# Making the token-independent S5 tables earlier and keeping them in DRAM, in a three-branch decoder layer on one core

## The chip, the core and the metric

The kernel runs on one core of a Trainium2 chip. The metric is the device time of one execution in microseconds (us), the median of several runs. A profiled execution lists every instruction of the engines: PE (TensorE; PEld is its weight load), DVE (VectorE), ACT (ScalarE), POOL (GpSimd), SP (SyncE, which here issues every DMA).

## What is computed

One layer over 2048 tokens of width 1024, all in float32. `h = RMSNorm(x)` goes through one input projection of 8716 columns, which is split among an S5 branch (`u_a`, `z_a`), an attention branch (`q`, `k`, `v`, `z_b`), a Mamba-2 branch (`xbc`, `dt`, `z_c`) and three merge gates. The S5 branch is the one that the change is about:

```python
def s5_mixer(u, a_re, a_im, log_step, b_re, b_im, c_re, c_im, d, glu_w, glu_b):
    step = jnp.exp(log_step.astype(f32))[:, None]
    mag = jnp.exp(a_re * step)
    ang = a_im * step
    lam_re, lam_im = mag * jnp.cos(ang), mag * jnp.sin(ang)
    ...                                            # bb = discretized b
    bu_re = jnp.einsum('gpi,bsgi->bsgp', bb_re, ug)
    bu_im = jnp.einsum('gpi,bsgi->bsgp', bb_im, ug)
    ...                                            # h_t = lam h_(t-1) + bu_t, complex, over 2048 tokens
    y = jnp.einsum('gip,bsgp->bsgi', c_re, h_re) - jnp.einsum('gip,bsgp->bsgi', c_im, h_im)
    y = y.reshape(Bt, S, S5_WIDTH) + d.astype(f32) * u
    g = jax.nn.gelu(y)
    return g * jax.nn.sigmoid(g @ glu_w + glu_b)
```

There are 32 groups of 16 channels with 64 complex states each. The powers of lambda, the discretized b and the products made of them depend on parameters alone, on no token.

## The kernel before

**The projection is the backbone.** `main` walks through 272 units of PE work, 136 for each half of the tokens. First half: 40 units of `main_qkv` (units 0 to 39), 12 of `main_dtz`, 20 of `main_xbc`, 16 of `main_uz` (72 to 87) and 48 of `main_gates` (88 to 135). Second half: 16 of `main_uz` (136 to 151), 40 of `main_qkv` (152 to 191), then the rest. A unit is 48 products of 128x256 or 24 of 128x512. Each 256 columns of weights (1 MB) come by `wload` (L339, tile `wr`, one buffer), and `wsplit` (L353) splits them on ACT (`wh`, L360) and DVE (`wl`, L361) into high and low parts, with six buffers for the eight half-tiles that two weights would need.

**Branch work is spread between the units.** `run` gets jobs (a generator, its number of steps, first unit, last unit) and advances each in proportion as the units pass. The framework then orders every engine's instructions by a simulated timeline, so the order on an engine is fixed when the program runs. All DMAs are issued in order by SP. Branch tiles come from pools that are opened and closed with the phases (`jp0`, `jp1`, `jp2`); the PSUM tiles of branch work share five banks (`cps`, L250).

**The S5 path.** `s5_setup` (L857, units 2 to 38) computes per-group tables over 128 partitions (real and imaginary part times 64 states) and writes them to `tab_d`, [128, 32 groups, 163 columns], in ten pieces of 16 to 19 columns (L935, L940, L952, L967, L1015). A piece of 16 columns lies in `tab_d` as runs of 64 bytes, one for each partition and group, 4096 runs to a piece.

`s5` (L1028, units 153 to 180 beside the second half's `main_qkv`) works in eight blocks of four groups. `prep` loads the block's tables and channels `u`, makes `x1` and `o0` (`cplx`: two POOL products and one DVE addition of 128x512 each, L1042 to L1044), from `o0` the lag kernels (`kp` on PE L1062, `ks` L1066 to L1068), writes these to `ks_d` and loads them back as a Toeplitz matrix `t0`. The block then transposes `x1` into `p1` (L1082), makes `o1` by `cplx`, and for each pair of groups the phasor table `wt` (four POOL products L1102 and L1103, two DVE operations L1104). None of these reads a token. For each group follow the token operations: a product `inc` (L1112), three DVE operations on it and a POOL addition (L1116 to L1119), the scan over 256 chunks on DVE (L1121), three more DVE operations and a POOL addition (L1127 to L1130), and two products into `yp` (L1132, L1133).

Beside the first half's gates run `ssd(0)` (units 73 to 135), which makes its decay matrices on POOL (`sr`, L806), and `a0_early` (units 84 to 120).

Of the kernel before, what the change touches and what calls it, by code (L numbers as in the profile page):

```python
# [21 lines left out]
P = 128  # L22
# [6 lines left out]
TABW = 163  # L29
# [4 lines left out]
class Small:  # L34
    """float32 exp, sin/cos and softplus on small parameter arrays, by range reduction and polynomials."""
# [94 lines left out]
    def softplus(self, x, out=None):  # L130
        """max(x, 0) + log1p(exp(-|x|)), log1p(e) = 2 atanh(e / (2 + e))"""
# [18 lines left out]
class Hybrid:  # L150
# [3 lines left out]
    # ---------------------------------------------------------------- memory  # L154
    def setup(self, ctx):
# [28 lines left out]
        self.tab_d = dram("tab_d", [P, 32, TABW])  # L184
# [21 lines left out]
        # additive attention mask [query, previous block | current block]  # L206
# [46 lines left out]
    # ------------------------------------------------------------- h^T  # L253
# [15 lines left out]
    def norm_tile(self, tt, xh, w=None):  # L269
        """rows of a token tile over their RMS (times w), transposed, in two halves"""  # L270
# [48 lines left out]
    def a0_early(self):  # L319
        """h^T of the second half, kept in DRAM until its first half is used up"""  # L320
# [16 lines left out]
    # ------------------------------------------------------- weight tiles  # L337
# [11 lines left out]
    def wtile(self, name, specs):  # L349
        """columns [(c0, n), ...] of w_in as fp32r hi and lo parts, four K-pairs each."""  # L350
# [15 lines left out]
    def tok_unit(self, wt, tb, tt, n, ps):  # L366
        """ps[tokens, n] = h w for token tile tt of time block tb."""
# [9 lines left out]
    def ch_unit(self, wt, tb, m, ps):  # L377
        """ps[channels, 512 tokens] = (h w)^T for the 128 columns m of a weight tile."""
# [16 lines left out]
    # -------------------------------------------------- the input projection  # L395
# [36 lines left out]
    def silu2(self, nm, z, out, zin=None):  # L432
        """out = 2 silu(z) = (tanh(z/2) + 1) z"""
# [49 lines left out]
    def conv(self, ct, tb, ps):  # L483
        """causal depthwise conv (weights halved), silu, and both layouts to DRAM"""
# [108 lines left out]
    class AttBlock:  # L593
        """one block of 128 queries, four heads, against its own and the previous block of keys"""
# [44 lines left out]
        def scores(self):  # L639
# [5 lines left out]
            # even and odd heads sit in different row halves of the array: one bank for each  # L645
# [40 lines left out]
    def merge(self):  # L686
        """mix of the three head groups by their softmax denominators, gate, y_b^T"""
# [35 lines left out]
    # ------------------------------------------------------------------ SSD  # L723
    def ssd_dt(self, half):
# [21 lines left out]
        # exact two-part split of dt * a for the one-pass products  # L746
# [109 lines left out]
    # ------------------------------------------------------------------- S5  # L856
    def s5_setup(self):  # L857
        """per-group tables over partitions (re | im, state): powers of lambda, phasors of lambda^8,
        discretized b and c in both complex arrangements"""
# [13 lines left out]
        tab = self.tab_d  # L873
        T = {}
# [65 lines left out]
        nc.sync.dma_start(tab[:, :, 147:163], w.rearrange("p g a n -> p g (a n)"))  # L940
# [5 lines left out]
        for i in range(2):  # L946
# [5 lines left out]
            nc.sync.dma_start(tab[:, :, 64 + 16 * i:80 + 16 * i], o)  # L952
# [8 lines left out]
        for i in range(2):  # L961
            pt = self.cps([P, 4, P], f"s5ct{i}")
            for b in range(4):
# [42 lines left out]
            # one step to modulus one: v (3 - |v|^2) / 2  # L1006
# [21 lines left out]
    def s5(self):  # L1028
# [5 lines left out]
        def cplx(b, w, name, kr, ki, x1, x2, f):  # L1034
            """[lr_n x1 +- li_n x2] over eight powers and 16 columns"""
            o = self.ct(f"s5{name}{b}", [P, 4, 8, 16], tag="s5c", bufs=5)
            t = self.ct(f"s5{name}t{b}", [P, 4, 8, 16], tag="s5ct", bufs=2)

            def bc(k, x):
                return (w[:, :, k:k + 8].unsqueeze(3).to_broadcast([P, 4, 8, 16]),  # L1040
                        x.unsqueeze(2).to_broadcast([P, 4, 8, 16]))
            gp.tensor_mul(o, *bc(kr, x1))  # L1042
            gp.tensor_mul(t, *bc(ki, x2))
            f(o, o, t)  # L1044
            return o

        def prep(b):
            gs = slice(b * 4, b * 4 + 4)
            w = self.ct(f"s5t{b}", [P, 4, TABW], tag="s5tab", bufs=2)
            nc.sync.dma_start(w, self.tab_d[:, gs, :])  # L1050
            u = self.ct(f"s5u{b}", [P, 4, 256], tag="s5u", bufs=2)
            for j in range(8):
                nc.sync.dma_start(u[j * 16:(j + 1) * 16],
                                  self.ua_d[b * 64:(b + 1) * 64, j, :].rearrange("(g i) c -> i g c", i=16))
            b1, b2, d1, d2 = (w[:, :, k:k + 16] for k in (64, 80, 96, 112))

            x1 = cplx(b, w, "x", 147, 155, b1, b2, v.tensor_add)
            o0 = cplx(b, w, "k", 128, 137, d1, d2, v.tensor_add)
            # lag kernels, zeros before lag 0, as rows of a Toeplitz matrix
# [11 lines left out]
            t0 = self.ct(f"s5t0{b}", [P, 4, P], tag="s5t0", bufs=2)  # L1071
            for i in range(8):
                nc.sync.dma_start(t0[i * 16:(i + 1) * 16], self.ks_d[:, gs, (7 - i) * 16:(7 - i) * 16 + P])
            return w, u, x1, d1, d2, t0

        todo = [prep(0)]
        yield
        for b in range(8):
            w, u, x1, d1, d2, t0 = todo.pop()
            pp = self.cps([P, 4, P], f"s5pp{b}")  # L1080
# [362 lines left out]
```

## Time and profile before

| what | us |
|---|---|
| time, median of 3 runs (2604.53 to 2605.4) | 2605.06 |
| span of the profiled execution | 2611.2 |
| PE busy in it | 2477.1 (95%) |
| DVE busy in it | 1465.2 (56%) |
| POOL busy in it | 718.3 (28%) |

The page of the profile cuts the span into 40 slices of 65.3 us, and its digits are busy shares in tenths. PE is at 9 nearly everywhere; it falls to 7 or 8 in the first four slices and again from the eighteenth to the twenty-first, where DVE stands at 8 and 9:

```profile
PE   8778999999999999978889999999999999999999
DVE  6652255643433335488986546642333887878663
```

### The profile page before, as it was taken

To read this page: it belongs to the slowest core of one execution; us is meant where nothing else is said; L and a number is where in the kernel's file an instruction comes from. 1 tells how busy PE (TensorE), PEld (TensorE's weight loads), DVE (VectorE), ACT (ScalarE), POOL (GpSimd) and SP (SyncE) were. 2 spreads that over 40 slices of the span, in tenths; PEclk is the share of its full clock that TensorE was granted. 3 is DMA by queue.
4 is the path that set the end of the run, shared out by engine and by line. 5 is a ranking of instruction groups with operands and counts; after the bars stand their busy time and mean duration, and the time that the engine had idled before them with its cause. 6 is when DMAs were issued, how large, how long until landed. Compare 5 with 4: busy or idle time off the path is not lost. (4 is left out here: it accounts for less than half of the span.)

```text
span 2611.2 us, 40810 instructions
## 1 busy us (share of the span) xinstructions
PE 2477.1 (95%) x15216; PEld 2173.1 (83%) x15216; DVE 1465.2 (56%) x3153; ACT 888.8 (34%) x1956; POOL 718.3 (28%) x737
## 2 busy tenths in 40 slices
PE   8778999999999999978889999999999999999999
PEld 8778998888888888877789998888888779797888
DVE  6652255643433335488986546642333887878663
ACT  4122234543233224212225335443332433333331
POOL 2121000002333324288862100000010343534221
PEclk8988999999999999999999999999999999999999
DMA  7995332433445335343336432443343667675664
GB/s 156 90 56 117 100 108 83 138 117 108 134 145 158 119 103 166 81 111 106 101 97 198 127 119 90 138 138 105 117 137 123 212 201 218 200 214 169 204 201 133
DMA packets 463591, 354.90 MB, mean 136 GB/s; under 512 B 132641, under 2 KB 420641, under 8 KB 463393
## 3 DMA queue, kind: packets, MB, share of 16 engines
q1 hardware_dynamic: 463392, 352.29, 50.6%
q8 instruction: 121, 1.98, 0.3%
q14 instruction: 78, 0.63, 0.1%
HBM read 239.79 MB, written 112.41 MB: 135 GB/s over the span
## 5 line engine op out<-in xcount | busy, mean ns | idle before, releaser
L384 PE MATMUL ps_g<-hT_hi,wh_g 128*128 128x512 f32 x768 | 310.0, 404 | 0.0
L386 PE MATMUL ps_g<-hT_hi,wl_g 128*128 128x512 f32 x768 | 305.6, 398 | 0.0
L385 PE MATMUL ps_g<-hT_lo,wh_g 128*128 128x512 f32 x768 | 305.0, 397 | 0.0
L806 POOL TENSOR_TENSOR sr<-tle,ahl 128x384 fp32r<-128x384 f32 x128 | 116.3, 930 | 519.9 <-PE sd L811 388.5
L386 PEld LDWEIGHTS ps_g<-hT_hi,wl_g 128*128 128x128 f32 x768 | 144.5, 188 | 33.1
L385 PEld LDWEIGHTS ps_g<-hT_lo,wh_g 128*128 128x128 f32 x768 | 144.5, 188 | 32.3
L384 PEld LDWEIGHTS ps_g<-hT_hi,wh_g 128*128 128x128 f32 x768 | 144.4, 188 | 32.2
L1272 POOL TENSOR_TENSOR fm<-fm,fg 128x512 f32<-128x512 f32 x64 | 96.0, 1500 | 209.7 <-DVE fg L1270 172.6
L361 DVE TENSOR_TENSOR wl_g<-wr_g,wh_g 128x512 fp32r<-128x512 f32 x96 | 71.0, 759 | 116.1 <-ACT wh_g L360 106.3
L659 ACT ACTIVATE sm<-sm,ml 128x256 f32<-128x256 f32 (+1 forms) x192 | 86.4, 451 | 136.1 <-DVE ml L657 111.9
L373 PE MATMUL ps_q<-wh_q,hT_hi 128*128 128x256 f32 x384 | 112.5, 294 | 18.0 <-ACT e_q L424 17.6
L384 PE MATMUL ps_xbc<-hT_hi,wh_xbc 128*128 128x512 f32 x320 | 129.0, 403 | 0.0
L385 PE MATMUL ps_xbc<-hT_lo,wh_xbc 128*128 128x512 f32 x320 | 128.6, 402 | 0.0
L386 PE MATMUL ps_xbc<-hT_hi,wl_xbc 128*128 128x512 f32 x320 | 128.4, 401 | 0.0
L373 PE MATMUL ps_v<-wh_v,hT_hi 128*128 128x256 f32 x384 | 110.7, 291 | 13.2 <-ACT e_v L414 10.8
L374 PE MATMUL ps_v<-wl_v,hT_hi 128*128 128x256 f32 x384 | 112.9, 295 | 9.5 <-DVE wl_v L361 9.5
L563 ACT ACTIVATE e_g<-ps_g 128x512 f32<-128x512 f32 x96 | 56.9, 595 | 182.3 <-PE ps_g L386 173.8
L498 DVE SCALAR_TENSOR_TENSOR ac_cv<-xb_cv,convw,ac_cv 128x512 f32<-128x512 f32 x120 | 90.3, 752 | 48.9 <-ACT ac_cv L496 48.2
L374 PE MATMUL ps_k<-wl_k,hT_hi 128*128 128x256 f32 x384 | 112.0, 292 | 5.8 <-DVE wl_k L361 5.7
L374 PE MATMUL ps_q<-wl_q,hT_hi 128*128 128x256 f32 x384 | 112.5, 294 | 4.6 <-DVE wl_q L361 4.6
L373 PE MATMUL ps_k<-wh_k,hT_hi 128*128 128x256 f32 x384 | 112.1, 294 | 4.8 <-ACT e_k L424 4.8
L375 PE MATMUL ps_q<-wh_q,hT_lo 128*128 128x256 f32 x384 | 113.4, 296 | 3.3 <-DVE hT_lo L317 3.3
(627 smaller groups left out, 7552.5 us busy)
## 6 DMA issues: line engine op xcount, KB each, us to landing
wr_g<-in_w_in_dram SPq DMA_DIRECT2D x24, 1024.0 KB, 5.3
g_d<-e_g SPq DMA_DIRECT2D x96, 256.0 KB, 2.4
fg<-g_d SPq DMA_DIRECT2D x96, 256.0 KB, 5.3
or<-in_w_out_dram SPq DMA_DIRECT2D x16, 1024.0 KB, 5.8
fr<-in_proj_c_dram SPq DMA_DIRECT2D x32, 384.0 KB, 5.1
wr_xbc<-in_w_in_dram SPq DMA_DIRECT2D x10, 1024.0 KB, 5.4
x<-in_x_dram SPq DMA_DIRECT2D x32, 256.0 KB, 3.9
wr_uz<-in_w_in_dram SPq DMA_DIRECT2D x8, 1024.0 KB, 5.4
```

The source lines that it names most:

```text
L361: nc.vector.tensor_sub(l[:, :, :n], s, h[:, :, :n].bitcast(F32))
L373: nc.tensor.matmul(ps, hi[:, t], wh, start=kt == 0, stop=False)
L374: nc.tensor.matmul(ps, hi[:, t], wl, start=False, stop=False)
L375: nc.tensor.matmul(ps, lo[:, t], wh, start=False, stop=kt == KT - 1)
L384: nc.tensor.matmul(ps, wh, hi, start=kt == 0, stop=False)
L385: nc.tensor.matmul(ps, wh, lo, start=False, stop=False)
L386: nc.tensor.matmul(ps, wl, hi, start=False, stop=kt == KT - 1)
L498: nc.vector.scalar_tensor_tensor(acc, xb[:, k:k + 512], cw[:, ct, k:k + 1], acc, op0=ALU.mult, op1=ALU.add)
L563: nc.scalar.activation(e, ps, AF.Tanh, scale=0.5)
L659: nc.scalar.activation(sm[:, h], sm[:, h], AF.Exp, bias=ml[:, h:h + 1], accum_out=ob[:, h, 64:65])
L806: nc.gpsimd.tensor_mul(r, self.tle.unsqueeze(1).to_broadcast([P, 3, P]), ahl[:, i, h0:h0 + 3].unsqueeze(2).to_broadcast([P, 3, P]))
L1272: nc.gpsimd.tensor_add(acc, acc, gt)
```

## The change

**Longer runs.** `tab_d` becomes [128, 8 blocks, 4 x 162]: within a block each piece holds its four groups side by side, so a piece of 16 columns is written by `put` as 1024 runs of 256 bytes in place of 4096 of 64. The decay `rho` leaves the table and goes to `rho_d`, 128 runs of 128 bytes. There are as many table writes as before and the bytes are the same.

**Tables earlier.** The parameter part of `s5` becomes `s5_tables`, 40 steps in units 83 to 134, beside `main_gates` of the first half, `ssd(0)` and `a0_early`. It runs the same POOL, DVE, PE and ACT operations and writes `p1`, `o1` (256 KB a block each) and `wt` (1 MB a block) to new DRAM tensors; `ks_d` is written as before. The pool `jp1` of the first attention is closed at unit 82 and `jp1t` is opened in its place; the steps of `ssd(0)` keep their pace.

**What is left of `s5`.** It has 42 steps in units 153 to 180. `load` fetches `u` (8 DMAs), `p1`, `wt`, `t0` (8) and `o1`, two buffers each, one block ahead. The token operations on PE, DVE, POOL and ACT are the same, one yield for each group. Elsewhere only comments and docstrings went.

```diff
-TABW = 163
+TABW = 162
...
-        self.tab_d = dram("tab_d", [P, 32, TABW])
+
+        self.tab_d = dram("tab_d", [P, 8, 4 * TABW])
+        self.rho_d = dram("rho_d", [P, 32])
+        self.p1_d = dram("p1_d", [P, 32, P])
+        self.o1_d = dram("o1_d", [P, 32, P])
+        self.wt_d = dram("wt_d", [P, 32, 2, 256])
...
-        tab = self.tab_d
-        T = {}
+        def put(off, wd, src):
+            nc.sync.dma_start(self.tab_d[:, :, off * 4:(off + wd) * 4], src)
...
-        w = self.ct("s5w", [P, 32, 19])
+        nc.sync.dma_start(self.rho_d, rho)
+        w = self.ct("s5w", [P, 32, 18])
         nc.vector.tensor_copy(w[:, :, 0:9], lr)
         nc.vector.tensor_copy(w[:, :, 9:18], li)
-        nc.vector.tensor_copy(w[:, :, 18], rho)
-        nc.sync.dma_start(tab[:, :, 128:147], w)
+        put(128, 18, w.rearrange("p (b g) k -> p b (g k)", b=8))
         w = self.ct("s5wr", [P, 32, 2, 8])
         for n in range(8):
             nc.vector.tensor_copy(w[:, :, 0, 7 - n], lr[:, :, n])
             nc.vector.tensor_copy(w[:, :, 1, 7 - n], li[:, :, n])
-        nc.sync.dma_start(tab[:, :, 147:163], w.rearrange("p g a n -> p g (a n)"))
+        put(146, 16, w.rearrange("p (b g) a n -> p b (g a n)", b=8))
...
-            nc.sync.dma_start(tab[:, :, 64 + 16 * i:80 + 16 * i], o)
+            put(64 + 16 * i, 16, o.rearrange("p (b g) k -> p b (g k)", b=8))
...
-            nc.sync.dma_start(tab[:, :, 96 + 16 * i:112 + 16 * i],
-                              d.rearrange("p b (g i) -> p (b g) i", i=16))
+            put(96 + 16 * i, 16, d.rearrange("p a (h c) -> p (a h) c", h=2))
...
-                k = 32 * lev + 16 * i
-                nc.sync.dma_start(tab[:, :, k:k + 16], ph[i])
+                put(32 * lev + 16 * i, 16, ph[i].rearrange("p (b g) k -> p b (g k)", b=8))
...
-    def s5(self):
+    def s5_tables(self):
...
+        for b in range(8):
             gs = slice(b * 4, b * 4 + 4)
+            w = self.ct(f"s5t{b}", [P, 4 * TABW], tag="s5tab", bufs=2)
+            nc.sync.dma_start(w, self.tab_d[:, b, :])
...
+            x1 = cplx("x", rev[:, :, 0:8], rev[:, :, 8:16], b1, b2)
+            pp = self.cps([P, 4, P], f"s5pp{b}")
+            for g in range(4):
+                nc.tensor.transpose(pp[:, g, :], x1[:, g].rearrange("p n i -> p (n i)"), self.ident)
+            p1 = self.ct(f"s5p1{b}", [P, 4, P], tag="s5p1", bufs=1)
+            nc.scalar.copy(p1, pp)
+            nc.sync.dma_start(self.p1_d[:, gs, :], p1)
+            yield
+            o0 = cplx("k", pw[:, :, 0:8], pw[:, :, 9:17], d1, d2)
...
             nc.sync.dma_start(self.ks_d[:, gs, :], ks.rearrange("p g n i -> p g (n i)"))
             yield
+            o1 = cplx("o", pw[:, :, 1:9], pw[:, :, 10:18], d1, d2)
+            nc.sync.dma_start(self.o1_d[:, gs, :], o1.rearrange("p g n i -> p g (n i)"))
+            yield
             for pr in range(2):
...
                     gp.tensor_mul(v16(wt[:, :, q, :]), hi16(32), lo16(x))
                     gp.tensor_mul(v16(tmp), hi16(48), lo16(y))
                     f(wt[:, :, q, :], wt[:, :, q, :], tmp)
+                nc.sync.dma_start(self.wt_d[:, b * 4 + pr * 2:b * 4 + pr * 2 + 2], wt)
                 yield
+
+    def s5(self):
+        nc = self.nc
+        v, gp = nc.vector, nc.gpsimd
+        rho = self.ct("s5rho", [P, 32])
+        nc.sync.dma_start(rho, self.rho_d)
+
+        def load(b):
+            gs = slice(b * 4, b * 4 + 4)
...
+            u = t4("u", None, (P, 4, 256))
+            for j in range(8):
+                nc.sync.dma_start(u[j * 16:(j + 1) * 16],
+                                  self.ua_d[b * 64:(b + 1) * 64, j, :].rearrange("(g i) c -> i g c", i=16))
+            p1 = t4("p1", self.p1_d[:, gs, :])
+            wt = t4("w", self.wt_d[:, gs], (P, 4, 2, 256))
+            t0 = t4("t0", None)
+            for i in range(8):
+                nc.sync.dma_start(t0[i * 16:(i + 1) * 16], self.ks_d[:, gs, (7 - i) * 16:(7 - i) * 16 + P])
+            return u, p1, wt, t0, t4("o1", self.o1_d[:, gs, :])
+
+        todo = [load(0)]
+        yield
...
-        run([(self.ssd(0), 66, 73, 135), (chain(self.attention(0, 0), self.attention(1, 0)), 40, 41, 80),
-             (self.a0_early(), 8, 84, 120)], 136)
+        ssd0, early0 = self.ssd(0), self.a0_early()
+        run([(early(ssd0, 10), 10, 73, 82), (chain(self.attention(0, 0), self.attention(1, 0)), 40, 41, 80)], 82)
+        s2.close()
+        s2, self.jp = open_pool("jp1t")
+        run([(ssd0, 56, 83, 135), (self.s5_tables(), 40, 83, 134), (early0, 8, 84, 120)], 136)
         s2.close()
         s1.close()
         st, self.jp = open_pool("jp2")
-        run([(self.s5(), 66, 153, 180)], 180)
+        run([(self.s5(), 42, 153, 180)], 180)
...
```

## Rows read from the trace of the kernel before

**Rows 1.** The page's first lines: span; busy us, share and instructions of engines.

```profile
span 2611.2 us, 40810 instructions
PE 2477.1 (95%) x15216; PEld 2173.1 (83%) x15216; DVE 1465.2 (56%) x3153; ACT 888.8 (34%) x1956; POOL 718.3 (28%) x737
```

**Rows 2.** Busy by stretch: PE, PEld, DVE, ACT, POOL (instructions), PEclk, DMA share, GB/s.

```profile
60.00:110.00 50.00, 49.56 (x420) 49.36 (x420) 40.92 (x249) 11.60 (x20) 7.82 (x8) 1.00 1.59 84
110.00:220.00 110.00, 68.67 (x480) 67.64 (x479) 41.53 (x166) 17.68 (x31) 18.75 (x16) 0.78 1.08 83
...
640.00:960.00 320.00, 320.00 (x1518) 262.44 (x1518) 116.32 (x158) 93.20 (x192) 107.55 (x122) 1.00 0.42 129
...
1100.00:1360.00 260.00, 217.28 (x1529) 201.31 (x1528) 232.56 (x354) 59.84 (x116) 218.53 (x217) 0.94 0.37 98
...
2000.00:2535.00 535.00, 502.70 (x2781) 429.71 (x2780) 412.93 (x790) 201.89 (x468) 199.16 (x164) 0.97 0.66 203
```

**Rows 3.** The same view of two short stretches in which PE never idles.

```profile
280.00:290.00 10.00, 10.00 (x88) 10.00 (x87) 1.38 (x2) 2.42 (x4) 0.00 (x0) 1.00 0.13 32
1000.00:1020.00 20.00, 20.00 (x88) 16.18 (x87) 10.82 (x10) 6.68 (x9) 17.82 (x15) 1.00 0.59 159
```

**Rows 4.** Waits of ACT from 110 to 220 us: total, times, longest.

```profile
ACT wh_k L360 <- DMA wr_k<-in_w_in_dram: 32.4, 1, 32.4
ACT wh_q L360 <- DMA wr_q<-in_w_in_dram: 31.4, 1, 31.4
ACT wh_v L360 <- DMA wr_v<-in_w_in_dram: 24.9, 1, 24.9
```

**Rows 5.** DMA in the same stretch: packets, megabytes, rate, packets by size.

```profile
DMA packets 29220, 9.16 MB, mean 83 GB/s; under 512 B 21663, under 2 KB 29215, under 8 KB 29215
```

**Rows 6.** DMA issues of the whole run: count, KB each, median us to landing.

```profile
wr_uz<-in_w_in_dram SPq DMA_DIRECT2D x8, 1024.0 KB, 5.4
...
ua_d<-e_uz SPq DMA_DIRECT2D x16, 256.0 KB, 2.6
...
tab_d<-s5ph SPq DMA_DIRECT2D x4, 256.0 KB, 17.6
```

**Rows 7.** Waits of PE from 1100 to 1360 us: total, times, longest.

```profile
PE s5kp L1062 <- DVE s5k L1044: 13.8, 4, 6.6
PE s5i L1112 <- DVE s5mt L1118: 9.3, 7, 2.0
PE s5yp L1132 <- DVE s5mt L1118: 6.7, 5, 2.2
```

**Rows 8.** DVE groups there: shapes, count, busy us, mean ns, idle before.

```profile
L1121 DVE TENSOR_TENSOR_SCAN s5h<-s5t,s5m 128x256 f32<-128x256 f32 x30 | 32.3, 1077 | 4.7 <-POOL s5m L1119 4.4 <-POOL s5r L1126 0.3
L1104 DVE TENSOR_TENSOR s5w<-s5w,s5wt 128x512 f32<-128x512 f32 x28 | 30.5, 1088 | 4.2 <-POOL s5w L1102 4.0
...
L1116 DVE TENSOR_TENSOR s5m<-s5i,s5w 128x256 f32<-128x256 f32 x30 | 12.5, 415 | 0.5
...
L1068 DVE SCALAR_TENSOR_TENSOR s5ks<-ident,s5dd,s5ks 16x16 f32<-16x16 f32 x28 | 9.0, 373 | 0.1
...
L1044 DVE TENSOR_TENSOR s5k<-s5k,s5kt 128x512 f32<-128x512 f32 x6 | 7.7, 1286 | 1.4 <-POOL s5kt L1043 1.4
...
L1044 DVE TENSOR_TENSOR s5o<-s5o,s5ot 128x512 f32<-128x512 f32 x6 | 4.6, 771 | 0.1
```

**Rows 9.** The scan's own line over the whole run: ns least, median, most.

```profile
L1121 DVE TENSOR_TENSOR_SCAN s5h<-s5t,s5m x32: 615/692/1597, 1091.9 to 1351.1; 128x256 f32<-128x256 f32 x32
```

**Rows 10.** POOL groups from 1100 to 1360 us, as in rows 8.

```profile
L1103 POOL TENSOR_TENSOR s5wt<-s5t 128x512 f32<-128x512 f32 x27 | 34.6, 1281 | 2.8 <-DVE s5w L1104 2.5
...
L1102 POOL TENSOR_TENSOR s5w<-s5t 128x512 f32<-128x512 f32 x28 | 34.1, 1239 | 0.0
...
L1042 POOL TENSOR_TENSOR s5x<-s5t 128x512 f32<-128x512 f32 x6 | 8.5, 1424 | 0.1
...
L1042 POOL TENSOR_TENSOR s5k<-s5t 128x512 f32<-128x512 f32 x6 | 7.3, 1215 | 0.0
```

**Rows 11.** ACT in order of time, 930 to 1000 us: start, duration, operation, idle before.

```profile
939.41 1.14 ACT L360 CAST wh_g<-wr_g 128x512 fp32r<-128x512 f32 x2 [3.60 <-DMA wr_g<-in_w_in_dram]
...
956.78 0.62 ACT L360 CAST wh_g<-wr_g 128x512 fp32r<-128x512 f32 x1 [3.20 <-PE ps_g L385]
```

More of the change, by code (lines that the diff above doesn't have):

```diff
@@ L1047, in prep, with piece, cplx, bc @@
-        def prep(b):
-            gs = slice(b * 4, b * 4 + 4)
[L1049 to L1058, printed above, removed]
+        for b in range(8):
+            gs = slice(b * 4, b * 4 + 4)
+            w = self.ct(f"s5t{b}", [P, 4 * TABW], tag="s5tab", bufs=2)
+            nc.sync.dma_start(w, self.tab_d[:, b, :])
+            def piece(off, wd=16):
+                return w[:, off * 4:(off + wd) * 4].rearrange("p (g k) -> p g k", k=wd)
+            pw, rev = piece(128, 18), piece(146)
+            b1, b2, d1, d2 = (piece(k) for k in (64, 80, 96, 112))
+            def cplx(name, lr, li, x1, x2):
+                o = self.ct(f"s5{name}{b}", [P, 4, 8, 16], tag="s5c", bufs=3)
+                t = self.ct(f"s5{name}t{b}", [P, 4, 8, 16], tag="s5ct", bufs=2)
+                def bc(k, x):
+                    return (k.unsqueeze(3).to_broadcast([P, 4, 8, 16]),
+                            x.unsqueeze(2).to_broadcast([P, 4, 8, 16]))
+                gp.tensor_mul(o, *bc(lr, x1))
+                gp.tensor_mul(t, *bc(li, x2))
+                v.tensor_add(o, o, t)
+                return o
+            x1 = cplx("x", rev[:, :, 0:8], rev[:, :, 8:16], b1, b2)
[7 more added lines that the diff above has]
+            o0 = cplx("k", pw[:, :, 0:8], pw[:, :, 9:17], d1, d2)
@@ L1070, in prep @@
             nc.sync.dma_start(self.ks_d[:, gs, :], ks.rearrange("p g n i -> p g (n i)"))
[L1071 to L1080, printed above, removed]
-            for g in range(4):
-                nc.tensor.transpose(pp[:, g, :], x1[:, g].rearrange("p n i -> p (n i)"), self.ident)
-            p1 = self.ct(f"s5p1{b}", [P, 4, P], tag="s5p1", bufs=2)
-            nc.scalar.copy(p1, pp)
-            o1 = cplx(b, w, "o", 129, 138, d1, d2, v.tensor_add)
             yield
-            yt = self.ct(f"s5y{b}", [P, 4, 256], tag="s5y", bufs=1)
+            o1 = cplx("o", pw[:, :, 1:9], pw[:, :, 10:18], d1, d2)
+            nc.sync.dma_start(self.o1_d[:, gs, :], o1.rearrange("p g n i -> p g (n i)"))
+            yield
             for pr in range(2):
@@ L1093, in lo16 @@
                 def lo16(k):
[L1094 removed]
+                    return piece(k)[:, g2].unsqueeze(2).to_broadcast([P, 2, 16, 16])
                 def hi16(k):
[L1097 removed]
+                    return piece(k)[:, g2].unsqueeze(3).to_broadcast([P, 2, 16, 16])
                 def v16(a):
@@ L1136, in s5, with t4 @@
-                if pr == 0 and b < 7:
-                    todo.append(prep(b + 1))
+    def s5(self):
[5 more added lines that the diff above has]
+            gs = slice(b * 4, b * 4 + 4)
+            def t4(name, src, shape=(P, 4, P)):
+                t = self.ct(f"s5{name}{b}", shape, tag=f"s5{name}", bufs=2)
+                if src is not None:
+                    nc.sync.dma_start(t, src)
+                return t
+            u = t4("u", None, (P, 4, 256))
[10 more added lines that the diff above has]
+        yield
+        lo, hi = slice(0, 64), slice(64, 128)
+        for b in range(8):
+            u, p1, wt, t0, o1 = todo.pop()
+            yt = self.ct(f"s5y{b}", [P, 4, 256], tag="s5y", bufs=1)
+            for g in range(4):
+                nm = f"{b}_{g}"
+                cs, sn = wt[:, g, 0, :], wt[:, g, 1, :]
+                inc = self.cps([P, 256], f"s5i{nm}")
+                nc.tensor.matmul(inc, p1[:, g, :], u[:, g, :], start=True, stop=True)
+                m = self.ct(f"s5m{nm}", [P, 256], tag="s5m", bufs=2)
+                t = self.ct(f"s5mt{nm}", [P, 256], tag="s5mt", bufs=2)
+                v.tensor_mul(m, inc, cs)
+                v.tensor_mul(t[lo], inc[hi], sn[hi])
+                v.scalar_tensor_tensor(t[hi], inc[lo], -1.0, sn[lo], op0=ALU.mult, op1=ALU.mult)
+                gp.tensor_add(m, m, t)
+                h = self.ct(f"s5h{nm}", [P, 256], tag="s5h", bufs=2)
+                gg = b * 4 + g
+                v.tensor_tensor_scan(h, rho[:, gg:gg + 1].to_broadcast([P, 256]), m, 0.0,
+                                     op0=ALU.mult, op1=ALU.add)
+                r = self.ct(f"s5r{nm}", [P, 257], tag="s5r", bufs=2)
+                rt = self.ct(f"s5rt{nm}", [P, 256], tag="s5mt", bufs=2)
+                gp.memset(r[:, 0:1], 0.0)
+                v.tensor_mul(r[:, 1:257], cs, h)
+                v.scalar_tensor_tensor(rt[lo], h[hi], -1.0, sn[hi], op0=ALU.mult, op1=ALU.mult)
+                v.tensor_mul(rt[hi], h[lo], sn[lo])
+                gp.tensor_add(r[:, 1:257], r[:, 1:257], rt)
+                yp = self.cps([P, 256], f"s5yp{nm}")
+                nc.tensor.matmul(yp, t0[:, g, :], u[:, g, :], start=True, stop=False)
+                nc.tensor.matmul(yp, o1[:, g, :], r[:, 0:256], start=False, stop=True)
+                nc.scalar.copy(yt[:, g, :], yp)
+                yield
+                if g == 1 and b < 7:
+                    todo.append(load(b + 1))
```

40 lines of the change are left out of this document (removed).

## The prediction

> **What bounds the kernel now.** I read the page's head first: PE is busy 2477 of 2611 us [rows 1], so the order of the day is PE's, and a change can only win where PE idles or runs at its lower clock. The view of busy times by stretch says where that is [rows 2]. From 110 to 220 us, the end of the first q, k, v units with `s5_setup` beside them, PE is busy 68.7 of 110 us at a granted clock of 0.78. From 1100 to 1360 us, the second half's q, k, v with `s5` beside them, it is busy 217.3 of 260 us at 0.94. From 640 to 960 us, the first half's gates with `ssd(0)`, it never idles, with DVE busy 116 and POOL 108 of 320 us. The change takes work from the first two and gives work to the third. The last stretch with gaps, 2000 to 2535 us, isn't touched.
>
> Next come the waits, to learn what holds PE in each. At 110 to 220 us ACT stands three times for 25 to 32 us before it can split a weight, always for the DMA that brings it [rows 4]; PE stands behind ACT. In that stretch 21663 of 29220 packets are under 512 bytes and the rate is 83 GB/s at a DMA share over 1 [rows 2, 5]: the queues are full of small writes, not of bytes. They are the table writes: one of 256 KB takes 17.6 us to land, against 5.4 us for a weight of four times the size [rows 6]. At 1100 to 1360 us PE waits longest for `o0` before the lag kernels (13.8 us), then for PSUM banks that late DVE operations hold (9.3 and 6.7) [rows 7]. DVE is busy 89% and POOL 84% there [rows 2].
>
> **Part A, longer runs.** Full speed is 88 instructions in 10 us [rows 3]; 480 instructions in 110 us [rows 2] are thus 54.5 us of work, and 55.5 us are lost. A table write becomes 1024 runs of 256 bytes. The row of the same form is the write of `ua_d`: 256 KB in runs of 256 bytes (64 columns), 2.6 us to land [rows 6]. Bounds for one write: 2.6 us, or 17.6 us if the run length did not matter; I take 2.6, since bytes, run and direction are all the same. (By count of runs alone it would be 17.6/4 = 4.4 us, which changes little.) Ten writes then cost 26 us of queue spread over some 130 us, and a weight behind one is late by 3 us. The extra write of `rho` is 128 runs, nothing beside these. What is late next is DVE: its 41.5 us would lie in some 55 us, 75%; from 60 to 110 us it was at 82% and PE lost 0.4 us to idling [rows 2]. I leave 6 us of stall: **A = 49 us**, bounds 0 and 55.
>
> The Trainium skill, "DMA: Bandwidth & Descriptors", section Specifications, wants 512 bytes or more for full rate and says that shorter transfers are read, changed and written back. By that rule the new runs of 256 bytes would still be slow, which is the third rival below. The trace agrees for 64 bytes (17.6 us) and shows little of it at 256 (2.6 us).
>
> **Part B, the S5 stretch without its tables.** Idle time is 260 - 217.3 = 42.7 us, and a clock of 0.94 costs 0.06 x 217 = 13 us: 55.7 us are to be had if PE never waits. PE's table work (transposes, lag kernels) moves and costs the same in the gates, so it cancels. POOL loses L1103 34.6, L1102 34.1 and six groups of L1042 and L1043 between 8.5 and 7.3, together 48.2 us [rows 10]: 218.5 - 117 = 102 us. DVE loses L1104 30.5, L1068 9.0 and three groups of L1044 (7.7 the largest, 4.6 the smallest), 20 us [rows 8]: 232.6 - 59 = 173 us. That stands beside some 200 us of PE, 87%, so DVE is late next. But it should shrink: the scan took 1077 ns in the mean [rows 8] and 692 in the median [rows 9], while L1116, which reads PSUM, took 415; halved POOL work gives back up to 30 x 0.385 = 11.6 us on the scan alone, and DVE stands at 161 us, 80%.
>
> What is added here: SP issues about as many DMAs a block as before (`p1`, `wt`, `o1` for the table load and the `ks_d` write), but 1.5 MB a block, 12 MB in all. The stretch moved 98 GB/s x 260 us = 25.5 MB; 37.5 MB in some 205 us are 183 GB/s, less than the 203 GB/s of 2000 to 2535 us [rows 2]. A weight behind a block's loads lands 1.5 MB / 203 GB/s = 7 us later; ACT and the q, k, v products behind it wait. I count that with the DVE stalls as 12 us. Bounds: 56 us, and 18 if only the 13.8 us wait for `o0`, with a third of the clock's loss, goes and every other wait stays. **B = 44 us**: nearer the upper end, since the waits in [rows 7] all hang on an engine that loses a quarter or half of its work.
>
> **Part C, the tables beside the gates.** PE never idles there, so nothing is won and something may be lost. POOL gets 117 x 32/28 = 134 us (the rows hold 28 of 32) and goes from 108 to 242 of 320 us, 75%; DVE gets 59 x 32/28 = 68 and goes from 116 to 184, 58%. ACT gets two small copies a block. DMA gets 12 MB of writes, 39 GB/s on 129 [rows 2], in long runs. Each block adds six issues to SP (table load, `p1`, `ks_d`, `o1`, two of `wt`); five of them wait for POOL or DVE results, and behind them in SP's order stand the gate weights and the gate stores. Also queued behind POOL's products are `ssd`'s `sr`, for which PE's decay products wait. Bounds: nothing, from 1000 to 1020 us, where the tables of the first blocks kept POOL busy 17.8 of 20 us and PE was full [rows 3]; or what 1100 to 1360 us shows at POOL 84%, 16% idle, 52 us of 320. I take **C = 8 us**: the first row has the same operations, but no `ssd` beside them. Closing and reopening the pool at unit 82 makes the first table load wait for the last attention block, which has ended by unit 80; free.
>
> **Sum.** 49 + 44 - 8 = 85 us: the profiled 2611 would become 2526. The span lies 6.1 us above the median; I take that to stay, so 2605 - 85 = **2520 us**.
>
> **The rivals.**
> First, S5 stays held by DVE: only the wait for `o0` goes (B = 18). For it: DVE at 80 to 87% of the time is about the 89% of now. Against: POOL falls to 52%, and the token chain no longer queues behind table products. 2605 - 49 - 18 + 8 = 2546 us with C as forecast.
> Second, POOL comes late beside the gates: PE's order is fixed, and each `sr` or PSUM bank that is late stops the gates too, at the worst 16% of 320 us (C = 52). For it: POOL at 75% with bursts of a block's 17 us. Against: [rows 3]. 2605 - 93 + 52 = 2564 us.
> The Trainium skill, "SBUF — State Buffer", section Who interferes with whom, says that a DVE instruction with two SBUF inputs and a POOL instruction that reads SBUF shut each other out for a whole instruction. That speaks against part C: were DVE held for all of the 134 us, it would stand at 318 of 320. The trace agrees in kind (415 ns with a PSUM input, 1077 for the scan beside POOL).
> Third, short runs stay slow by the byte, so the longer runs do not do what they say: A = 0, 2605 - 44 + 8 = 2569 us. Against: `ua_d`.
> Fourth, slower: SP stands at table writes that wait for POOL, with the gate weights behind. A gate weight's first half is split from 939.41 us, and its last parts wait until 956.78 us for the old weight's buffers [rows 11], so it may come some 16 us late. It decides from there: if a block's two batches of POOL work (2 x 17 us) hold SP, each block costs 34 - 16 = 18 us, 144 in all: 2605 - 93 + 144 = 2656 us.
>
> **Chances.** Forecast 0.66, first rival 0.14, second 0.10, third 0.04, fourth 0.06. The forecast with its bounds spans 2496 (A 55, B 56, C 2) to 2545; reaching to the first two and part of the third the range is 2496 to 2568. A measurement of this kernel can tell 0.2%, some 5 us, from no change. All but the fourth are faster by more; I give 0.92 faster, 0.02 the same (a mild form of the fourth), 0.06 slower.
>
> **What would show it.** A: table writes land in under 5 us, ACT's waits for weights from 110 us on fall under 8 us each, and PE reaches its 220 us point near 170. B: the stretch of the S5 token work shrinks from 260 to some 205 us, no wait for `o0`, clock back near 1.0. C: the gates stay at full PE, POOL near 75%. Wrong would be: PE waits for `sr` or for a gate weight between 600 and 930 us (second and fourth), PE idle over 25 us beside the S5 token work (first), or table writes over 10 us (third).

## The result, and the profile after

The changed kernel takes **2524.57 us** (median of 4 runs, 2521.45 to 2531.67) against 2604.8 us (2603.34 to 2605.4) for the kernel before beside it: a ratio of 0.9692, 95% interval [0.9677, 0.9707], 80 us. The forecast was 2520 (2496 to 2568). The sum of the steps came out within 5 us. Two of its three terms were about 4 us too small and the third, a loss, 13 us too small, so the errors partly cancel.

The head of the page and two of its rows of 40 slices (63 us each), to set beside [rows 1]. Line numbers are those of each kernel's own file: L360 before is L365 after.

```profile
span 2521.8 us, 40932 instructions
PE 2450.7 (97%) x15216; PEld 2148.9 (85%) x15216; DVE 1440.9 (57%) x3152; ACT 887.3 (35%) x1956; POOL 710.8 (28%) x737
...
PE   8999999999999999999999999999999999998999
...
DVE  6942545537445533377765455622335887878663
```

The span fell by 89.4 us: PE's idle time (span less PE busy) from 134.1 to 71.1 us, that is 63.0, and PE's busy time by 26.4 with as many matmuls, nearly all because the clock is higher (the clock losses below fall by 22 us). The holes of PE near slices 2 to 4 and 18 to 21 are gone.

Busy times by stretch, as in [rows 2] (PE, PEld, DVE, ACT, POOL with instructions; PEclk, DMA share, GB/s). The third and fourth rows are the gates with the table steps, the last is the S5 token work, which before lay from 1100 to 1360 us:

```profile
60.00:110.00 50.00, 50.00 (x426) 50.00 (x425) 46.35 (x266) 15.16 (x26) 10.15 (x10) 1.00 0.40 115
110.00:220.00 110.00, 110.00 (x932) 110.00 (x931) 53.54 (x174) 31.40 (x53) 31.30 (x31) 1.00 0.39 119
...
560.00:850.00 290.00, 273.84 (x1297) 220.08 (x1296) 164.88 (x213) 85.06 (x177) 215.54 (x199) 0.98 0.54 171
850.00:985.00 135.00, 135.00 (x634) 109.83 (x633) 58.85 (x82) 44.94 (x80) 45.65 (x47) 1.00 0.46 150
1060.00:1265.00 205.00, 199.13 (x1506) 191.88 (x1506) 152.14 (x289) 53.97 (x106) 97.05 (x132) 1.00 0.55 156
```

From 110 to 220 us PE now never idles, and 932 matmuls fit where 480 did. The S5 stretch has 1506 matmuls in 205 us, before 1529 in 260. But the gates, where PE was full [rows 2], now hold 16 us of idle time at a clock of 0.98.

DMA issues of the whole run (count, KB each, median us to landing), beside [rows 6]:

```profile
wt_d<-s5w SPq DMA_DIRECT2D x16, 512.0 KB, 2.8
...
tab_d<-s5ph SPq DMA_DIRECT2D x4, 256.0 KB, 3.3
tab_d<-s5d SPq DMA_DIRECT2D x2, 256.0 KB, 7.7
```

A table write lands after 3.3 us in place of 17.6. The two of `s5d` go out at 55 us, among the kernel's first loads. ACT's waits for weights from 110 to 220 us (total, times, longest), which were 25 to 32 us long [rows 4]:

```profile
ACT wh_v L365 <- DMA wr_v<-in_w_in_dram: 9.5, 2, 4.8
ACT wh_q L365 <- DMA wr_q<-in_w_in_dram: 6.4, 1, 6.4
ACT wh_k L365 <- DMA wr_k<-in_w_in_dram: 4.9, 1, 4.9
```

How short writes make a weight late shows in SP's own order in the kernel before (start, us, what):

```profile
99.40 9.85 SPq L952 DMA_DIRECT2D tab_d<-s5bb  x2
109.34 11.95 SPq L417 DMA_DIRECT2D v_d<-e_v  x2
121.38 0.42 SPq L345 DMA_DIRECT2D wr_k<-in_w_in_dram  x1
```

SP spent 21.8 us on issuing four writes before it could issue the load of the weight that ACT then waited 32.4 us for. After, the same four take 1.2 and 6.0 us and the load goes out at 97.81 us.

All waits of PE from 500 to 1060 us, where it had none to speak of before:

```profile
PE xT L292 <- DVE x L286: 8.5, 6, 3.2
PE syd L825 <- DVE sm L819: 3.4, 1, 3.4
PE spt L856 <- DVE sx L850: 2.1, 3, 1.4
PE ps_g L389 <- ACT e_g L568: 2.1, 1, 2.1
```

They add up to 16.1 us, the whole idle time there. None names `sr`, a gate weight or a table: PE stands at the transposes of `a0_early` (`xT`) and at `ssd(0)` (`syd`, `spt`). What lies behind one of these, the 3.4 us of `syd`, stands in the chain of waits, followed back from 690 us (start, us, what):

```profile
664.45 1.02 POOL s5x L1057
665.47 1.02 POOL s5wt L1102
...
667.17 1.40 POOL s5ot L1058
668.56 0.52 POOL xs L243
...
669.10 1.06 DVE x L286
...
670.77 0.60 DVE s5w L1103
671.37 2.08 DVE wl_g L366 x2
...
673.47 8.05 DMA wr_g<-in_w_in_dram
...
681.60 0.63 ACT wh_g L365
...
684.00 0.48 DVE sm L819
...
684.53 1.47 PE syd L825 x6
```

Table products on POOL come first, with an `xs` factor of `a0_early` behind them. DVE's `x` waits for that factor, and the table's subtraction (L1103) and the old weight's last low parts (`wl_g`) stand behind `x` in DVE's order. Only when these have read the one `wr` buffer can SP fetch the next gate weight, at 673.47. ACT waits for that in order, and `ssd`'s `sm` lies behind the split. ACT and SP in that stretch (560 to 850 us), one view each:

```profile
ACT wh_g L365 <- DMA wr_g<-in_w_in_dram: 58.3, 9, 9.6
```

```profile
SPq L1104 <- DVE s5w L1103: 51.9, 11, 10.8
SPq L350 <- DVE wl_g L366: 35.1, 8, 6.8
```

L1104 is the write of `wt`, where SP stands up to 10.8 us, with weight loads behind it.

Beside the S5 token work only this wait of PE over 1 us is left, and the scan runs at one speed (ns least, median, most), where its mean was 1077 [rows 8, 9]:

```profile
PE s5yp L1164 <- POOL s5r L1161: 5.4, 5, 2.0
```

```profile
L1152 DVE TENSOR_TENSOR_SCAN s5h<-s5rho,s5m x32: 678/691/694, 1065.6 to 1256.6; 128x256 f32<-128x256 f32 x32
```

**Where the time went.** Idle time and clock loss (PE busy times one less the granted clock) of each phase, added up over windows of 5 us; the phases run between three landmarks, the first store of `dt`, the last store of `ua` and the last copy of `s5y`:

| phase | before: idle, clock | after: idle, clock | gain |
|---|---|---|---|
| 60 us to the first `dt` (319.7; after 264.2) | 41.8, 11.7 | 0, 0 | 53.5 |
| gates to the last `ua` (1033.1; 1014.0) | 0, 0 | 16.2, 4.6 | -20.8 |
| from there to the last `s5y` (1358.7; 1261.2) | 42.7, 11.0 | 5.9, 0 | 47.8 |
| from there to the end | 39.8, 13.2 | 39.5, 9.0 | 4.5 |

That makes 85.0 of the span's 89.4 us; 1.5 more lie before 60 us.

### The profile page after: what moved, and what is told of

It reads as the page before. It is cut to its first block, busy times and chain, and to the rows that moved or that the text cites. A ratio compares the mean times of both kernels' runs of the same rounds, so it can differ in the third digit from the quotient of the medians.

```text
span 2521.8 us, 40932 instructions
## 1 busy us (share of the span) xinstructions
PE 2450.7 (97%) x15216; PEld 2148.9 (85%) x15216; DVE 1440.9 (57%) x3152; ACT 887.3 (35%) x1956; POOL 710.8 (28%) x737
## 4 chain that ended last, share of the span: by engine, by line
PE 71%; DMA 9%; DVE 9%; POOL 5%; issue 3%; SPq 2%; ACT 1%; DVEq 0%; POOLq 0%; ACTq 0%
PE ps_g L389 5%; PE ps_g L391 5%; PE ps_g L390 5%; PE ps_xbc L390 3%; PE ps_xbc L391 3%; PE ps_xbc L389 3%; PE ao L685 3%; PE as L656 2%; PE ps_uz L389 2%; PE ps_uz L390 2%; PE ps_uz L391 2%; PE ps_q L380 2%; PE ps_q L379 2%; PE ps_q L378 2%; PE op L1335 1%
## 5 line engine op out<-in xcount | busy, mean ns | idle before, releaser
L811 POOL TENSOR_TENSOR sr<-tle,ahl 128x384 fp32r<-128x384 f32 x128 | 121.6, 971 | 415.9 <-PE sd L816 281.9
L366 DVE TENSOR_TENSOR wl_g<-wr_g,wh_g 128x512 fp32r<-128x512 f32 x96 | 77.1, 823 | 109.2 <-ACT wh_g L365 104.4
L498 POOL COPY halo<-xb_cv 128x3 f32<-128x3 f32 x40 | 8.5, 212 | 358.6 <-ACT xb_cv L497 358.6
L380 PE MATMUL ps_v<-wh_v,hT_lo 128*128 128x256 f32 x384 | 108.1, 282 | 0.0
```

The costliest lines, as they stand in the source:

```text
L366: nc.vector.tensor_sub(l[:, :, :n], s, h[:, :, :n].bitcast(F32))
L380: nc.tensor.matmul(ps, lo[:, t], wh, start=False, stop=kt == KT - 1)
L811: nc.gpsimd.tensor_mul(r, self.tle.unsqueeze(1).to_broadcast([P, 3, P]), ahl[:, i, h0:h0 + 3].unsqueeze(2).to_broadcast([P, 3, P]))
```

## The experiments

Times are medians; a ratio is to the kernel before in the same rounds, and a gain in us is that ratio applied to the median of the kernel before. "Idle time in the gates" is PE's from 500 us to the last store of `ua`; with the clock loss of the same stretch it makes the loss in the gates, which is 20.8 us in the table above.

**Longer runs alone** (`s5` as before).

```diff
-        self.tab_d = dram("tab_d", [P, 32, TABW])
+        self.tab_d = dram("tab_d", [P, 8, 4 * TABW])
+        self.rho_d = dram("rho_d", [P, 32])
...
+                put(32 * lev + 16 * i, 16, ph[i].rearrange("p (b g) k -> p b (g k)", b=8))
```

> The kernel before with the long runs alone (part A); the S5 tables stay beside the second half's q, k, v. Theory: the stall of the first 220 us comes from the table writes in 64-byte runs, so this alone wins what the landmarks of the two profiles show up to the first store of the dt units (319.7 to 264.2 us): 55 us, 2605 to about 2550 us, with the S5 stretch as before (PE idle some 43 us). Rival: the first stretch is faster because the planner ordered everything anew with the moved tables; then the gain here is under 30 us.

2551.95 us, ratio 0.9838 [0.9814, 0.9863]: 42 us where 55 were expected. The time expected came because the kernel before took 2596 us in these rounds, not 2605. Its table writes (`s5ph`) land after 3.3 us; the gates and the S5 stretch in the view of busy times:

```profile
640.00:960.00 320.00, 320.00 (x1502) 261.90 (x1501) 118.43 (x161) 100.14 (x194) 106.54 (x116) 1.00 0.43 136
1040.00:1300.00 260.00, 223.00 (x1573) 205.82 (x1572) 229.40 (x362) 61.77 (x120) 209.09 (x217) 0.96 0.36 98
```

Its first `dt` store comes at 263.9 us, as in the whole change, so part A is this edit alone. The S5 stretch still idles 37 us, and the gates idle not at all: the loss there comes with the tables, not with the earlier start.

**Tables earlier, with the old short runs.**

```diff
-        self.tab_d = dram("tab_d", [P, 8, 4 * TABW])
+        self.tab_d = dram("tab_d", [P, 32, TABW])
-            nc.sync.dma_start(self.tab_d[:, :, off * 4:(off + wd) * 4], src)
+            nc.sync.dma_start(self.tab_d[:, :, off:off + wd], src)
```

> The changed kernel with the table writes back in 64-byte runs (parts B and C alone). Theory: the parts act in different stretches and add up, so this wins 80 - 55 = 25 to 34 us, about 2574 us, and the first 220 us stall as before. Rival: the two parts share one gain (a table that is late holds the work that reads it); then this alone wins over 45 us and the sum of the two parts is well over the whole.

2557.08 us, ratio 0.9853 [0.9836, 0.9869]: 38 us, between the 25 to 34 of the theory and the 45 of the rival. The early stretch is slow again, through the writes:

```profile
tab_d<-s5ph SPq DMA_DIRECT2D x4, 256.0 KB, 13.8
```

```profile
110.00:220.00 110.00, 86.76 (x663) 85.74 (x662) 48.02 (x176) 24.32 (x43) 24.25 (x22) 0.89 0.76 98
```

Up to the first `dt` store (296.7 us) idle time and clock cost 31.5 us here. Idle time in the gates is 13.4 us (20.8 with the clock), beside the S5 token work 4.9. The two halves, 42 and 38 us, stand against 80, 70 and 71 us for the whole in three other sets of rounds: they add up, as far as these sets agree with each other. No set has the halves and the whole side by side.

**The kernel before, profiled again**, in other rounds.

> The kernel before unchanged, for a second profile on this chip. In the first profile of it the 64-byte table writes took 17.6 us (s5ph) to 23.2 us (s5bb) and cost 55 us of the first 220; with early tables and short runs on another chip they took 13.8 and 17.4 us and cost 32. If the cost of such writes differs from one chip or execution to another, this profile shows the shorter times (about 14 us and 17 us, first dt store near 297 us). If the pitch of the table's rows (652 against 648 bytes) or the order makes the difference, it shows the first profile's (first dt store near 320 us).

```profile
tab_d<-s5ph SPq DMA_DIRECT2D x4, 256.0 KB, 15.9
```

2600.53 us. The same 4096 runs land after 15.9 us in place of 17.6 (13.8 in the run above), and the first `dt` store comes at 305.0, not 319.7; idle time and clock to that point cost 41.2 us, not 53.5. With long runs it came between 263.9 and 265.1 us in every profile. So part A was worth 53.5 us in the execution on which the prediction rests and 41 in this one. The two spans differ by 12.5 us (2611.2 and 2598.7), and 12.3 of them are this stall; the first span also lies above every timed run of its own rounds (2603.34 to 2605.4). The result falls between the two cases that were expected. It shows that the cost varies for one and the same kernel; whether the chip or the execution decides is open, and the row pitch may add to it.

**The changed kernel beside it**, in the same rounds.

> The changed kernel unchanged, on this chip and in the same rounds as the version with both moves, so that the two can be compared. About 0.969 of the kernel before.

2528.61 us, ratio 0.973 [0.9713, 0.9747]: 70 us, less than the 0.969 expected. Between this pair the first `dt` comes 40.8 us earlier, the gates lose 36.3 and the S5 phase wins 78.1 by the landmarks, against 55.5, 36.4 and 78.4 for the pair of the result (these include PE's own table work and some of the projection's, which change place). What differs between the two pairs is mostly part A: 14.7 of the 17.6 us by which the gains in span differ. In the gates the idle time is 14.9 us, 20.9 with the clock.

**Runs of 128 bytes**, with each block's table loaded in ten pieces.

```diff
-        self.tab_d = dram("tab_d", [P, 8, 4 * TABW])
+        self.tab_d = dram("tab_d", [P, 16, 2 * TABW])
-            nc.sync.dma_start(self.tab_d[:, :, off * 4:(off + wd) * 4], src)
+            nc.sync.dma_start(self.tab_d[:, :, off * 2:(off + wd) * 2], src)
```

> The changed kernel with the tables written in runs of 128 bytes (2048 to a table of 256 KB) in place of 256; each block's table is then loaded in ten pieces. If the cost goes by the count of runs, a write lands after about 17.6/2 = 8.8 us (7 to 9 with what 4096 runs took in the other runs, 13.8 to 17.6); if it goes by bytes until a threshold above 128 bytes, it stays at 14 to 18 us; if the short runs are dear at 64 bytes alone, about 3.3 us. First store of dt: some 264 us if writes land in under 5 us, towards 280 otherwise.

```profile
tab_d<-s5ph SPq DMA_DIRECT2D x4, 256.0 KB, 7.3
```

1024 runs take 3.3 us, 2048 take 7.3, 4096 take 13.8 to 17.6: from 64 to 256 bytes the same 256 KB cost by the count of runs, 3.2 to 4.3 ns each. The Trainium skill, "DMA: Bandwidth & Descriptors", section Specifications, puts the limit of efficient transfers at 512 bytes. No write here has runs of 512 bytes, so that limit is not tested, but runs of 256 are still dear by the byte: 512 KB in 128 runs of 4 KB (`wt_d`) landed after 2.8 us. The time is 2526.59 us (one run) and the first `dt` store comes at 264.5, not towards 280 as expected for writes over 5 us: at 7.3 us they already keep out of the weights' way, so runs of 128 bytes would have given all of part A.

The other runs go after the loss in the gates.

**Tables spread over more units**, twice, the second time beside the changed kernel.

```diff
-        run([..., (self.s5_tables(), 40, 83, 134), (early0, 8, 84, 120)], 136)
+        run([..., (self.s5_tables(), 40, 83, 150), (early0, 8, 84, 120)], 152)
```

> The changed kernel with the table steps spread over units 83 to 150 in place of 83 to 134, so that a fourth of them falls beside the second half's u, z units, where POOL is idle. Theory: the 16 us of PE idle time and the lower clock from 560 to 850 us come from POOL being 74% busy, so that results behind it come late; at some 60% the idle time falls to about 6 us and the time to some 2512 us. Rival: what the gates lose is the tables' own PE work and bank use, which moves with the tables: then the time stays within 4 us of 2524.

> The tables spread over units 83 to 150, as once before, now beside the changed kernel in the same rounds. Theory: 5 to 8 us below the changed kernel, idle time in the gates about 8 us, as before. Rival (the earlier difference was the chip's): within 3 us of the changed kernel.

> The changed kernel itself, the measure for the other two of these rounds: 2522 to 2530 us, idle time in the gates 15 to 16 us.

2518.93 us, ratio 0.9704 [0.9688, 0.972]; in the later rounds 2521.13 [0.9697, 0.9723] against 2526.74 [0.9709, 0.9742] for the changed kernel: some 5 us, with intervals that still overlap. Idle time in the gates is 8.1 us in both, 12.8 in the changed kernel beside it, where 15 to 16 were expected (12.8 and 11.1 with the clock, against 20.7). The first spread run missed its 2512 us and came near its 6 us of idle time; the second fell 5.6 us below the changed kernel, as expected. The later two from 560 to 850 us, spread first:

```profile
560.00:850.00 290.00, 281.85 (x1341) 227.40 (x1340) 168.69 (x205) 86.66 (x179) 207.70 (x193) 0.99 0.53 167
```

```profile
560.00:850.00 290.00, 277.15 (x1301) 223.19 (x1300) 165.51 (x213) 85.35 (x177) 216.35 (x200) 0.97 0.55 172
```

**`a0_early` taken from beside the tables** to units 42 to 78.

```diff
-        run([(early(ssd0, 10), 10, 73, 82), (chain(...), 40, 41, 80)], 82)
+        run([(early(ssd0, 10), 10, 73, 82), (chain(...), 40, 41, 80), (early0, 8, 42, 78)], 82)
-        run([..., (early0, 8, 84, 120)], 136)
+        run([...], 136)
```

> The changed kernel with a0_early (the second half's norm and transposes) moved from units 84 to 120 to units 42 to 78, beside the first attention, away from the tables. Theory: PE's largest wait in the gates is for the normed x tiles, whose row factors queue behind the table products on POOL; without them there the idle time of 16 us halves and the time is about 2516 us. Rival: the attention stretch, where DVE is busier, loses as much: 2524 or more.

2521.25 us, ratio 0.9714 [0.97, 0.9729], where about 2516 was expected; the changed kernel was not timed in these rounds, and its ratios of 0.9692 to 0.973 elsewhere lie on both sides. The profile is clearer: idle time in the gates is 8.3 us, the loss with the clock 11.1, while five profiles with `a0_early` and the tables in the places of the changed kernel have 20.3 to 20.9. By stretch, and PE's waits from 500 to 1015 us:

```profile
560.00:850.00 290.00, 282.49 (x1327) 228.16 (x1326) 173.05 (x201) 72.42 (x136) 230.99 (x201) 0.99 0.47 152
```

```profile
PE spt L856 <- DVE sx L850: 4.9, 3, 3.6
PE syd L825 <- DVE sm L819: 2.7, 2, 2.4
```

The wait at `xT` is gone, half the loss with it, although POOL is busier there than in the changed kernel (231 us of 290 against 216; over all of the gates, 500 to 1015 us, it is 269 against 271). From 720 to 800 us POOL is busy 67.9 us here and PE never idles; in the changed kernel it is busy 57.5 us and PE idles 3.8. POOL's share of the time is not what sets the loss. What is queued behind its table products fits, but the run took away all of `a0_early`, its PSUM tiles and its work on ACT and DVE too.

**Both moves at once** (`a0_early` in units 58 to 90, tables in 86 to 150).

> The changed kernel with a0_early moved to units 58 to 90 and the table steps spread over units 86 to 150. Theory: no PE wait for normed x tiles and little for late POOL results is left in the gates (idle under 5 us of the 16), and the time is 8 to 14 us under that of the changed kernel in the same rounds. Rival: the earlier place of a0_early costs what the gates win, as the conv units also need ACT and DVE; then the difference is under 4 us.

2519.87 us, ratio 0.9698 [0.968, 0.9716], 8.7 us below the changed kernel in its rounds. Idle time in the gates is 10.6 us (14.4 with the clock) where under 5 was expected: the moves don't add. One late block of `a0_early` costs 6.2:

```profile
PE xT L292 <- DVE x L286: 6.2, 1, 6.2
```

**The phasor tables' additions on POOL in place of DVE.**

```diff
-                for q, (x, y, f) in enumerate(((0, 16, v.tensor_sub), (16, 0, v.tensor_add))):
+                for q, (x, y, f) in enumerate(((0, 16, gp.tensor_sub), (16, 0, gp.tensor_add))):
```

> The changed kernel with the last step of each phasor table (the 32 additions and subtractions of 128x512 that DVE made of two POOL products) given to POOL itself: DVE no longer stands in its order behind these products, but POOL gets 32 x about 1.2 us = 38 us more beside the gates (215 to some 250 of 290 us). Theory (the gates lose because DVE, and through it the low parts of the gate weights and SP's next weight load, stand in order behind POOL-fed table work): the waits of the gate weights vanish, PE's idle time from 500 to 1015 us falls from 15 to 16 us to under 10, and the time falls by 5 to 10 us below the changed kernel's of the same rounds. Rival (POOL as a whole is too busy beside the gates): idle time grows to 25 us or more and the time rises by 10 us or more.

```profile
560.00:850.00 290.00, 267.88 (x1268) 215.96 (x1267) 151.49 (x181) 84.96 (x175) 238.32 (x222) 0.97 0.54 169
```

```profile
PE xT L292 <- DVE x L286: 14.6, 7, 5.4
PE spt L856 <- DVE sx L850: 7.2, 5, 2.4
```

2533.91 us, ratio 0.9754 [0.9738, 0.9771], 7.2 us over the changed kernel of these rounds; idle time in the gates 22.1 us against 12.8, and with the clock 27.8 against 20.7, which is the whole difference in time. The theory, that DVE's standing behind POOL's products is the root, falls: DVE no longer stands there and the loss grew. The rival had the direction right and the size too large. With additions among the products each table holds POOL for longer, and the `x` and `sx` chains behind it come later: `xT` waits 14.6 us in place of 7.4. That fits a delay that begins in POOL's own order and is passed on by DVE and SP, as far as one edit tells: POOL also has more work here, and other work was ordered anew for it.

**Without the tables' products on PE** (the transposes into `p1` and the lag kernels are left out, so S5's output is not computed; the copies read other data).

> The changed kernel with the tables' transposes and lag kernel products left out on PE (p1 and ks are copied from x1 and o0 by the same ACT operations; POOL, DVE and DMA work stay), so it doesn't compute S5's output. It measures what of the 36 us that the first half's gates gave back, by the landmark of the last ua store, is PE's own moved table work. Theory: 10 to 16 us earlier than 1014 us at the last ua store, with about the same 16 us of idle time. Rival: the idle time comes from the tables' PE instructions and banks waiting in PE's order for POOL; then the idle time falls under 6 us and the last ua store comes 25 us or more earlier.

```profile
560.00:850.00 290.00, 240.48 (x1072) 194.23 (x1071) 183.94 (x214) 78.91 (x162) 224.28 (x197) 0.89 0.51 160
```

```profile
PE xT L292 <- DVE x L286: 27.9, 6, 18.9
PE spt L856 <- DVE sx L850: 20.3, 3, 17.3
```

2559.52 us (one run): with less work on PE it is some 31 us slower than the changed kernel on that chip. Both expectations missed. Idle time in the gates is 49.5 us, clock loss 15. With those products gone the engines are ordered anew, and ACT stands at the copies that now wait for the tables' DVE results, with the splits of gate weights and the `x` tiles behind it in order (12.9 us of waiting from 560 to 850 us at the copy of `ks` alone).

PE's table work, for which the run was made, follows only by subtraction: the last `ua` store comes 29.6 us later (1043.7 against 1014.1) with 43.6 us more lost, so some 14 us of PE work are gone, an estimate. The run does show that the tables' other operations beside the gates, in another order, cost three times as much.

Together, from 560 to 850 us: POOL busy 197, 208, 216, 224, 231 and 238 us (both moves, spread, changed, without PE products, `a0_early` moved, POOL additions) stand beside an idle time in the gates of 11, 8, 13 to 16, 50, 8 and 22 us. It doesn't follow POOL's share.

## Why the prediction was right, and where its steps were not

**Part A, 49 us: right in mechanism, a little low.** The writes land in 3.3 us (2.6 taken from `ua_d`), and the 6 us of stall left for DVE don't come: DVE is at 53.5 of 110 us. 53.5 us were won in idle time and clock. The signs named for it came: ACT's waits are under 7 us, and PE is 55.5 us ahead at the first `dt` store; of the writes only the two of `s5d` stayed over 5 us (7.7). But the term is the property of one execution: it was 41 us in another (the second pair), which no single profile could tell. The 3.3 us lie between the 2.6 that were taken and the 4.4 "by count of runs", and from 64 to 256 bytes the count is what is paid. It changed little.

**Part B, 44 us: right, a little low.** 47.8 us won. The stretch went to 205 us with DVE at 74% (80% forecast), POOL at 47% (52%), 156 GB/s (183). The scan's mean fell from 1077 to about 690 ns, as the step on POOL's share assumed. The 12 us left for DVE and the loads are 5.9, and what is late last is POOL's addition before `yp`, not DVE.

**Part C, 8 us lost: mis-sized; 20.8 were lost.** POOL's 75% and DVE's 58% were forecast and came out as 74% and 57%, yet PE stood idle. The step that failed is the choice of the lower bound's row: from 1000 to 1020 us [rows 3] POOL was as busy with the same products, but neither `ssd` nor `a0_early` was queued behind them. The run with `a0_early` taken away halves the loss (20.8 to 11.1 us), and with the tables left in the second half there is none. The text had named `sr` and the gate weights as what would be late, and PE's waits for them as the sign of being wrong; the first never shows, the second only through ACT, so the loss came without its sign. `a0_early`, on which half of the loss hangs, it left out of the list of what is queued past POOL's products. The second rival's mechanism (POOL late) and a mild form of the fourth (SP at the table writes, weights behind) are thus both there, at 21 us together in place of 52 or 144. The rule of the Trainium skill's "SBUF — State Buffer", section Who interferes with whom, was weighed against part C with DVE held for all of POOL's time; that much does not show, for DVE stands at 57%, as the sum without it had it. Single operations do agree with the rule: the table's subtraction, which reads two SBUF tiles, took twice its shortest time in the median beside POOL's products (ns least, median, most; the second line is the kernel with runs of 128 bytes):

```profile
L1103 DVE TENSOR_TENSOR s5w<-s5w,s5wt x32: 677/1306/1959, 568.7 to 867.8; 128x512 f32<-128x512 f32 x32
L1105 DVE TENSOR_TENSOR s5w<-s5w,s5wt x32: 673/693/1957, 564.0 to 868.2; 128x512 f32<-128x512 f32 x32
```

In the second kernel it mostly ran at its shortest, and the gates lost 20.3 us all the same, so these longer operations alone don't set the loss.

**The sum.** 49 + 44 - 8 = 85 against 53.5 + 47.8 - 20.8 = 80.5: the errors of +4.5 and +3.8 made up for two thirds of the miss of 12.8. Two smaller things cancelled as well: 4.5 us less idle time and clock loss after the S5 phase, which no step had, and the profile's offset. The span before lay 6.1 us above its median and I let that stay; after, it lies 2.8 below. By spans the forecast was 2526 and 2521.8 came. By the second profile of the kernel before, whose span differs from the first by part A alone, the offset is most likely part A's too, so that its 49 us fitted a slower execution than the timed ones. In two other sets of rounds the change was worth 70 and 71 us, not 85: that the forecast came within 5 us is in part luck.

**The rivals.** First, S5 held by DVE: refuted by 5.9 us of idle time. Third, runs slow by the byte: refuted by 3.3 us, and by the run with longer runs alone. Second and fourth: present, small.

**What stays open.** No run separates POOL's order from SP's; a second `wr` buffer might, and was not tried. That the `xs` factor's place behind table products is what makes `a0_early` late was read from one chain; no run moved that factor alone. Why the order without PE's table products costs 49.5 us is seen in its waits only. The best versions seen are both moves (2519.9 us) and the tables spread to unit 150 (2518.9 and 2521.1); in their own rounds they lie 8.7 and 5.6 us under the change, at the edge of what can be told.

## What to carry to other kernels

When a write to DRAM stands in the way of loads, count its runs: the same 256 KB cost 3.3, 7.3 or 13.8 to 17.6 us at 1024, 2048 or 4096 of them, and at 7 us PE lost next to nothing to them here (0.3 us). Work moved beside a stretch in which PE never idles was not paid here by the share of its engine's time but, as far as the runs show, by what stands in order behind each piece of it; list every job that runs there, the small ones too, and look for a row of the trace that holds all of them before a loss is called nothing. And a term read from one profile may be worth a quarter less in the next execution, so a second profile of the kernel before is worth more than a finer sum.

## What the hardware showed that was not expected

The time of the short writes is not a constant: 256 KB in runs of 64 bytes landed after 17.6 and 15.9 us in two profiles of the kernel before, and the stall that they caused was 53.5 and 41.2 us (idle and clock, up to the first `dt` store). In the kernel with early tables and short runs they were 13.8 and 31.5 us. The same bytes in runs of 256 took 3.3 us in every profile (`s5ph`). The clock's share was larger than a table of idle times suggests: between the two profiles PE's busy time fell by 26.4 us for equally many matmuls, while its idle time fell by 63.0 and the granted clock from 110 to 220 us rose from 0.78 to 1.00.
